# A 1-core encoder layer: four operands of the second token pair split while gate and up are computed, and other statistics at three places

## The chip, the core and the metric

The kernel runs on one core of one Trainium2 chip. The metric is the device time of one execution in microseconds (us), the median of several executions. Engines are named as in the profile: PE (TensorE), DVE (VectorE), ACT (ScalarE), POOL (GpSimd), SP (SyncE, which issues most DMAs). All arithmetic is fp32.

## What is computed

One layer of an encoder for 1088 tokens (64 of a running stream, 1024 of a new prompt), 1024 features, hidden width 2816:

```python
h = rmsnorm(x, g_mix)
z = h @ w_in                       # columns: u (512), v (512), xb (512)
ya = gelu(u) * gmlp_spatial(rmsnorm(gelu(v), g_v), w_s, b_s)
yb, new_hist = pool_mix(xb, hist, start_pos, w_pool, pool_scale)
x = x + concat(rmsnorm(ya), rmsnorm(yb)) @ w_out
h = rmsnorm(x, g_ffn)
x = x + (silu(h @ w_gate) * (h @ w_up)) @ w_down
y = rmsnorm(x, g_final)
```

`rmsnorm` divides each token by the root of its mean square over the features. The results are y, the pooling history and the normalised v of the running stream.

## The kernel before

Activations lie feature-major: 128 features on the partitions, tokens along the row. PE has no full-speed fp32 product, so every factor is split in a high part (a cast by ACT) and a low part (a subtraction by DVE), and every product is three matmuls: high x high, high x low, low x high (`passes`, L90; `products`, L659).

**Start.** L224 to L249 load x in eight feature tiles, split each, and form the sum of squares per token: ACT squares a tile (L205), POOL adds it to `sqx` (L206, `square_add`). PE computes v for six of the token tiles as x arrives, then the seventh (L249). `rstd` (L125) then sums `sqx` over the partitions with nine one-column matmuls (L128), DVE scales the sums (L130), POOL raises them to the power -1/2 (L132). Its PSUM bank is one of eight that are handed out in turn.

**Output projection.** The tokens are worked in two halves of 544 ("pairs", x = 0 and x = 1), each of two quarters of 272 (Q). After each half the second norm is made by `prep(x)` (L562), a generator whose pieces are advanced between other work: `stat` (L479: one-column matmuls L484, DVE L489, POOL power L491), `row` (L494: five transposes L497 that turn the statistic into a row along the tokens, copied out of PSUM by L498), the scaling L573, and seven operands of a Strassen-Winograd 2x2 scheme, each cast (L578) and subtracted (the helper `sub`, L471). They stand in `R0` for x = 0 and `R1` for x = 1. Order of use: B11, T1, T2, B21, T3, B22, T4; as numbers B11, T3, B21, B22 are 0 to 3, and T1, T2, T4 are 4 to 6. `R1[0..3]` are in tiles `Yh`, `Yl`.

**Gate and up.** 22 units j of 128 hidden columns (`gu_unit`). Each calls `products`, seven products of 12 matmuls per half (L678); after five of the products PSUM is read out: ACT copies (`grab`, L692), DVE adds and subtracts, ACT applies silu (L711, L716), DVE writes the result `G` (L718, L719). After every odd unit `g_operands` forms the seven operands that the down projection needs from two units and stores them in DRAM (`gd`, L731). Weights come through `load_w` (three DMAs, L613 to L615, which take three buffers "F" from `f_free`) and `steps` (DVE sums and differences of weight blocks, ACT cast L626, DVE subtraction), into pairs of buffers `w_free`; `fill` runs steps as long as a pair is free.

**Down.** The hidden pairs are summed in three groups (4, 4, 3). A group has four units q (two output tiles each); its 14 operands are fetched from `gd` (`g_load`, L819, one DMA of 544 KB each) into the low tile and split there (`g_split`, L823 by ACT and L471 by DVE). `g_next` does this for the next group, product by product, as the last unit of the group before (which is run once per half) lets each operand go. The sums are held in `accC`, `accE`, `accL`.

**End.** `finish(x)` (L914): `stat`, `row`, eight scalings L921 and eight DMAs L922.

Within each engine the order is fixed by a scheduler when the program is built; each engine runs its own instructions in that order, and SP issues its DMAs in that order too.

Of the kernel before, what the change touches and what calls it, by code (L numbers as in the profile page):

```python
# [58 lines left out]
def encoder_kernel(ctx: ExitStack, tc: tile.TileContext, xT, w_in, w_out, w_gu, w_down,  # L59
# [139 lines left out]
    def square_add(acc, x, c, first, scale=1.0):  # L199
        a, e = c  # L200
        if first:
            nc.scalar.activation(acc[:, a:e], x, AF.Square, scale=scale)
        else:
            t = tmp()
            nc.scalar.activation(t[:, 0:e - a], x, AF.Square, scale=scale)  # L205
            nc.gpsimd.tensor_tensor(out=acc[:, a:e], in0=acc[:, a:e], in1=t[:, 0:e - a], op=ALU.add)  # L206
# [21 lines left out]
    for k in range(KT):  # L228
        raw = xr[k // 4][:, k % 4]
        parts = ((0, mid), (mid, T)) if k < 2 else ((0, T),)  # L230
        if k < 2:
            nc.sync.dma_start(wr[:, k], w_in[0, 0][:, k])
        for a, e in parts:
            nc.sync.dma_start(raw[:, a:e], xT[k][:, a:e])
        if k < 2:
            split(wr, *vw[0], g_mix[:, 0:2], (k,))
        for a, e in parts:
            nc.scalar.copy(Hh[k][:, a:e], raw[:, a:e])
            nc.vector.tensor_tensor(out=Hl[k][:, a:e], in0=raw[:, a:e], in1=f(Hh[k][:, a:e]), op=ALU.subtract)
        for c in CH:  # L240
            square_add(sqacc, raw[:, c[0]:c[1]], c, k == 0)
        if k % 2 and k < 6:
            vw.append(weights(0))
        for b in first_tiles:
            passes(vps[b], tok_pairs(vw, (k,), b), k == 0, k == KT - 1)

    nc.sync.dma_start(gv_b, g_rows[0].partition_broadcast(P))
    ps = bank()
    passes(ps, tok_pairs(vw, range(KT), 7))  # L249
    vps[7] = ps  # L250
    r1 = rstd(sqacc, D, "x")
# [227 lines left out]
    def stat(sums, dim, name):  # L479

        ps = bank()
        for i, o, n in BLOCKS:
            for k, (a, at) in enumerate(sums):
                nc.tensor.matmul(ps[0:n, i:i + 1], a[:, at + o:at + o + n], ones, start=k == 0, stop=k == len(sums) - 1)  # L484
# [3 lines left out]
        for i, j, n in ((0, q - 1, P), (q - 1, q, BLOCKS[-1][2])):  # L488
            nc.vector.tensor_scalar(out=m[0:n, i:j], in0=ps[0:n, i:j], scalar1=1.0 / dim, scalar2=EPS,  # L489
# [4 lines left out]
    def row(r, out):  # L494
        R = bank2().rearrange("p a t -> p (a t)")
        for i, o, n in BLOCKS:
            nc.tensor.transpose(R[:, o:o + n], r[0:n, i:i + 1].to_broadcast([n, P]), ident[0:n, 0:n])  # L497
        nc.vector.tensor_copy(out, R[:, 0:2 * Q])  # L498

# [222 lines left out]

    def g_operands(p, xs):
# [6 lines left out]
        def store(c, v, n=2):  # L730
            nc.sync.dma_start(gd[p, c:c + n, :, a:e].rearrange("c p x t -> p c x t"), v)  # L731
# [80 lines left out]
    fill()  # L812
    make_R1()
    pieces = prep(1)


    def g_load(c, base, J, x):
        h, l = (t[:, 0:J] for t in RR[x][c])
        nc.sync.dma_start(f(l), gd[base:base + J, c, :, x].rearrange("j p t -> p j t"))  # L819
# [6 lines left out]
    def g_next(base, J, x):  # L826

        def between(c):
            g_load(c, base, J, x)
            g_split(c, J, x)  # L830
        return between

    gx = dram.tile([P, 2, Q], F32, name="gx")
    kept = []
    for i, (j, xs, how) in enumerate(units):
        if i == 3:
            for _ in pieces:
                pass
            e = big.tile([P, 2, 2, HALF], F32, tag="E", name="F")
            wx = big.tile([P, 2, 2, HALF], F32R, tag="Hl67", name="W")  # L840
            extra = [e[:, 0], e[:, 1]]
            f_free += extra
            extra_w = (wx[:, 0], wx[:, 1])
            w_free.append(extra_w)
        if i == len(units) - 5:
            retired[:] = [id(slot) for slot in extra + c_pairs]
            give(f_free, [])
# [4 lines left out]
        elif i == 2:  # L852
            gu_unit(j, xs, lambda c: next(pieces, None), kept=kept)
            nc.sync.dma_start(gx, G[1][:, :, 1])
        elif i < len(units) - 1:
            gu_unit(j, xs, lambda c: next(pieces, None), **(dict(keep=kept) if how else {}))
# [13 lines left out]
    def acc_tiles():  # L870
        c = big.tile([P, 4, T], F32, tag="C", name="accC")
        e = big.tile([P, 2, T], F32, tag="E", name="accE")
        acc[0:6] = [c[:, 0], c[:, 1], c[:, 2], c[:, 3], e[:, 0], e[:, 1]]
        for m in range(6):
            acc_load(m)

    def acc_last():
        retired[:] = [id(extra_w)]
# [35 lines left out]
    def finish(x, last):  # L914
        r = stat([(sq3, 2 * Q * x)] + [(t, 0) for t in last], D, f"o{x}")
        yield
        R = tmp2()
        row(r, R)
# [99 lines left out]
```

## Time and profile before

| | us |
|---|---|
| median of the runs shown (3) | 1036.54 |
| lowest, highest | 1034.67, 1038.34 |
| the profiled execution | 1037.52 |
| its span, first to last instruction | 1035.7 |
| PE busy | 1004.0 (97% of the span) |
| DVE, ACT, POOL busy | 649.2 (63%), 415.5 (40%), 102.8 (10%) |
| mean granted TensorE clock | 0.979 |
| bytes moved by DMA | 131.34 MB |

The page of the profile gives busy times, the span in 40 slices and the chain of work that ended last. Three other views of the same trace are used below: busy time by stage (one line for each stretch of the span), waits (which engine sat idle, until which instruction, how often, the longest), and the timeline (single instructions in order). "Busy" for PE is modelled, so that a full stretch can still run at the lower of its two clock levels, 1.2 instead of 2.4 GHz; the column PEclk, the granted clock as a share of the upper level, shows it.

### The profile page before, as it was taken

Reading aid. Unit: us, or ns where it says so; the run is one execution under the profiler, and the core shown is the slowest. Engines: PE = TensorE matmul, PEld = TensorE weight load, DVE = VectorE, ACT = ScalarE, POOL = GpSimd, SP = SyncE. Lnnn points to the kernel's source line nnn. Section 1 sums busy time; section 2 is a strip of 40 time slices with the busy share of each in tenths; the row PEclk is TensorE's granted clock in tenths of the full one; section 3 lists DMA queues with packets and bytes.
Section 4 is the critical chain, followed back from the end, with each engine's and each line's share of the span. In section 5 each row is a group of like instructions: output and inputs, shape, how many; then the busy total and the mean of one; then the engine's idle time right before and its main releaser. Section 6 shows DMA issues by size and latency. Waiting matters only on the chain.

```text
span 1035.7 us, 17622 instructions
## 1 busy us (share of the span) xinstructions
PE 1004.0 (97%) x7355; PEld 976.4 (94%) x7355; DVE 649.2 (63%) x871; ACT 415.5 (40%) x634; POOL 102.8 (10%) x117
## 2 busy tenths in 40 slices
PE   8899999999989999999999999999989998999994
PEld 7789988999989999999999999999989998999994
DVE  6658628435888455655545655455596579559855
ACT  7373435322444333333333333333473264236530
POOL 6630141112300000000000000000000000000320
PEclk9999999999989999999999999999999999999996
DMA  8211101997614231613323134153584283236104
GB/s 305 72 41 50 42 31 42 361 319 261 197 43 140 72 117 42 206 41 127 118 71 117 53 115 130 39 184 106 175 277 132 70 259 121 77 97 192 54 1 172
DMA packets 71792, 131.34 MB, mean 127 GB/s; under 512 B 7009, under 2 KB 31073, under 8 KB 71713
## 3 DMA queue, kind: packets, MB, share of 16 engines
q1 hardware_dynamic: 70560, 128.00, 37.6%
q10 hardware_dynamic: 1152, 2.23, 0.6%
q8 instruction: 57, 0.93, 0.4%
q14 instruction: 23, 0.18, 0.1%
HBM read 90.98 MB, written 39.22 MB: 126 GB/s over the span
## 4 chain that ended last, share of the span: by engine, by line
PE 87%; DVE 4%; DMA 2%; issue 1%; ACT 1%; POOL 0%; DVEq 0%; ACTq 0%
PE ps L678 63%; PE ps L95 21%; DMA R0l<-gd 1%; PE ps L484 1%; DVE Yl L471 0%; DMA R1l<-gd 0%; DVE R1l L471 0%; DVE accL L474 0%; PE ps L497 0%; PE ps L418 0%; DVE X1a L573 0%; DVE Wl L471 0%; PE ps L141 0%; ACT Yh L578 0%; ACT t L692 0%
## 5 line engine op out<-in xcount | busy, mean ns | idle before, releaser
L678 PE MATMUL ps<-R0h,Wh 128*128 128x272 f32 x624 | 182.2, 292 | 4.4 <-ACT t L692 1.8
L678 PE MATMUL ps<-R0h,Wl 128*128 128x272 f32 x624 | 180.6, 290 | 0.1
L678 PE MATMUL ps<-R0l,Wh 128*128 128x272 f32 x624 | 180.1, 289 | 0.0
L471 DVE TENSOR_TENSOR Wl<-F,Wh 128x1024 fp32r<-128x1024 f32 (+2 forms) x96 | 102.8, 1073 | 77.6 <-ACT Wh L626 77.6
L692 ACT COPY t<-ps 128x544 f32<-128x544 f32 (+1 forms) x172 | 87.7, 514 | 152.3 <-PE ps L678 149.9
L626 ACT CAST Wh<-F 128x1024 fp32r<-128x1024 f32 (+3 forms) x96 | 87.6, 912 | 148.3 <-PE ps L678 132.9
L678 PEld LDWEIGHTS ps<-R0h,Wh 128*128 128x128 f32 x624 | 118.1, 189 | 6.6 <-ACT t L692 3.8
L678 PE MATMUL ps<-R0h,W 128*128 128x272 f32 x568 | 121.2, 294 | 3.1 <-ACT t L692 3.1
L678 PEld LDWEIGHTS ps<-R0l,Wh 128*128 128x128 f32 x624 | 118.3, 190 | 0.0
L678 PEld LDWEIGHTS ps<-R0h,Wl 128*128 128x128 f32 x624 | 117.7, 189 | 0.3 <-DVE Wl L471 0.3
L545 POOL TENSOR_TENSOR sq<-sq,t 128x544 f32<-128x544 f32 x20 | 34.7, 1745 | 747.9 <-PE ps L678 670.9
L678 PE MATMUL ps<-Yh,Wh 128*128 128x272 f32 x352 | 102.6, 292 | 4.0 <-DVE G L718 2.2
L678 PE MATMUL ps<-Yh,Wl 128*128 128x272 f32 x352 | 102.2, 290 | 0.0
L678 PE MATMUL ps<-Yl,Wh 128*128 128x272 f32 x352 | 101.7, 289 | 0.0
L678 PEld LDWEIGHTS ps<-R0h,W 128*128 128x128 f32 x568 | 95.5, 193 | 3.5 <-ACT t L692 3.5
L678 PE MATMUL ps<-R1h,Wh 128*128 128x272 f32 x280 | 82.1, 293 | 1.0 <-ACT t L692 1.0
L678 PE MATMUL ps<-R0l,W 128*128 128x272 f32 x284 | 83.0, 292 | 0.0
L678 PE MATMUL ps<-R1h,Wl 128*128 128x272 f32 x280 | 81.6, 292 | 0.0
L678 PE MATMUL ps<-R1l,Wh 128*128 128x272 f32 x280 | 81.1, 290 | 0.0
L474 DVE TENSOR_TENSOR t<-ps,t 128x544 f32<-128x544 f32 (+1 forms) x50 | 32.8, 655 | 70.6 <-PE ps L678 70.6
L678 PE MATMUL ps<-Yh,W 128*128 128x272 f32 x352 | 73.6, 290 | 0.1
L471 DVE TENSOR_TENSOR F<-F 128x512 f32<-128x512 f32 (+1 forms) x105 | 71.9, 699 | 1.2
(253 smaller groups left out, 2423.4 us busy)
## 6 DMA issues: line engine op xcount, KB each, us to landing
gd<-G SPq DMA_DIRECT2D x30, 544.0 KB, 3.7
F<-in_w_gu SPq DMA_DIRECT2D x46, 256.0 KB, 2.7
F<-in_w_gu SPq DMA_DIRECT2D x23, 512.0 KB, 3.9
R0l<-gd SPq DMA_DIRECT2D x14, 544.0 KB, 5.3
raw<-in_w_in SPq DMA_DIRECT2D x11, 512.0 KB, 3.9
t<-in_xT SPq DMA_DIRECT2D x16, 272.0 KB, 4.8
Yl<-gd SPq DMA_DIRECT2D x8, 544.0 KB, 5.3
raw<-in_w_out SPq DMA_DIRECT2D x8, 512.0 KB, 5.6
```

The source lines that it names most:

```text
L95: nc.tensor.matmul(ps, a, b, start=first and i == 0, stop=last and i == n - 1)
L471: nc.vector.tensor_tensor(out=o, in0=a, in1=b, op=ALU.subtract)
L474: nc.vector.tensor_tensor(out=o, in0=a, in1=b, op=ALU.add)
L484: nc.tensor.matmul(ps[0:n, i:i + 1], a[:, at + o:at + o + n], ones, start=k == 0, stop=k == len(sums) - 1)
L545: nc.gpsimd.tensor_tensor(out=a, in0=a, in1=t, op=ALU.add)
L626: nc.scalar.copy(h, F[:, 0:k])
L678: nc.tensor.matmul(ps[:, x, 0:Q], w[:, half, k * P:(k + 1) * P], v[:, k], start=start and i == 0, stop=i == 3 * K - 1, skip_group_check=True)
L692: nc.scalar.copy(t, ps)
```

## The change

1. `square_add` works on two chunks of 544 tokens, not three of 364, 362 and 362.
2. `rstd` of x stands ahead of the seventh token tile's matmuls.
3. `stat` sums over its k sources outermost, each matmul into a column of its own; DVE then sums the columns (two TENSOR_REDUCE, L490) ahead of the scaling, which is unchanged in count. `row` is divided: `row_ps` leaves the row in PSUM, and the last `finish` reads it there, eight times, with no copy.
4. A tile `ES` takes the place of two weight buffers (`f_free` has four in place of six). From the fourth unit on, where both halves are at hand, operands 0 to 3 of half x = 1 are split by `store` as they are made (four casts, four subtractions of 272 columns for a hidden pair) and both parts are stored in a new DRAM tensor `gs`; `gd` receives their x = 0 part. At the changes of group these four are fetched already split, two DMAs of 544 KB (408 KB for the third group) in place of one DMA, one cast and one subtraction of all four (three) hidden pairs.
5. The statistic of `prep(1)` is emitted before the first unit; its seven other pieces are advanced at every second product of the first two units, not at every one. A `fill` ahead of them is gone. `accE` is allocated and loaded one unit later.

The number of matmuls of the products is unchanged.

```diff
--- before.py
+++ after.py
@@ -201,7 +201,7 @@
         if first:
             nc.scalar.activation(acc[:, a:e], x, AF.Square, scale=scale)
         else:
-            t = tmp()
+            t = tmp2()
             nc.scalar.activation(t[:, 0:e - a], x, AF.Square, scale=scale)
             nc.gpsimd.tensor_tensor(out=acc[:, a:e], in0=acc[:, a:e], in1=t[:, 0:e - a], op=ALU.add)
 
@@ -237,7 +237,7 @@
         for a, e in parts:
             nc.scalar.copy(Hh[k][:, a:e], raw[:, a:e])
             nc.vector.tensor_tensor(out=Hl[k][:, a:e], in0=raw[:, a:e], in1=f(Hh[k][:, a:e]), op=ALU.subtract)
-        for c in CH:
+        for c in ((0, 2 * Q), (2 * Q, T)):
             square_add(sqacc, raw[:, c[0]:c[1]], c, k == 0)
         if k % 2 and k < 6:
             vw.append(weights(0))
@@ -245,10 +245,10 @@
             passes(vps[b], tok_pairs(vw, (k,), b), k == 0, k == KT - 1)
 
     nc.sync.dma_start(gv_b, g_rows[0].partition_broadcast(P))
+    r1 = rstd(sqacc, D, "x")
     ps = bank()
     passes(ps, tok_pairs(vw, range(KT), 7))
     vps[7] = ps
-    r1 = rstd(sqacc, D, "x")
     prefetch(2)
 
 
@@ -479,22 +479,28 @@
     def stat(sums, dim, name):
 
         ps = bank()
-        for i, o, n in BLOCKS:
-            for k, (a, at) in enumerate(sums):
-                nc.tensor.matmul(ps[0:n, i:i + 1], a[:, at + o:at + o + n], ones, start=k == 0, stop=k == len(sums) - 1)
+        for k, (a, at) in enumerate(sums):
+            for i, o, n in BLOCKS:
+                nc.tensor.matmul(ps[0:n, 8 * k + i:8 * k + i + 1], a[:, at + o:at + o + n], ones, start=True, stop=True)
         q = len(BLOCKS)
         m = const.tile([P, q], F32, name=f"m_{name}")
         r = const.tile([P, q], F32, name=f"r_{name}")
         for i, j, n in ((0, q - 1, P), (q - 1, q, BLOCKS[-1][2])):
-            nc.vector.tensor_scalar(out=m[0:n, i:j], in0=ps[0:n, i:j], scalar1=1.0 / dim, scalar2=EPS,
+            v = ps[0:n, 0:8 * len(sums)].rearrange("p (k i) -> p i k", i=8)[:, i:j]
+            nc.vector.reduce_sum(out=m[0:n, i:j], in_=v, axis=mybir.AxisListType.X)
+            nc.vector.tensor_scalar(out=m[0:n, i:j], in0=m[0:n, i:j], scalar1=1.0 / dim, scalar2=EPS,
                                     op0=ALU.mult, op1=ALU.add)
             nc.gpsimd.tensor_tensor(out=r[0:n, i:j], in0=m[0:n, i:j], in1=mhalf[0:n, i:j], op=ALU.pow)
         return r
 
-    def row(r, out):
+    def row_ps(r):
         R = bank2().rearrange("p a t -> p (a t)")
         for i, o, n in BLOCKS:
             nc.tensor.transpose(R[:, o:o + n], r[0:n, i:i + 1].to_broadcast([n, P]), ident[0:n, 0:n])
+        return R
+
+    def row(r, out):
+        R = row_ps(r)
         nc.vector.tensor_copy(out, R[:, 0:2 * Q])
 
 
@@ -720,6 +726,11 @@
 
         products(HALF, xs, after, between, **how)
 
+
+
+    gs = dram.tile([NF // 2, 4, 2, P, Q], F32, name="gs")
+    ES = []
+
     def g_operands(p, xs):
 
         a, e = xs[0], xs[-1] + 1
@@ -728,6 +739,16 @@
         t4 = tmp2().rearrange("p (x t) -> p x t", x=2)[:, a:e]
 
         def store(c, v, n=2):
+            if ES and e == 2 and c < 4:
+                hl = ES[0][:, c // 2]
+                for i in range(n):
+                    nc.scalar.copy(hl[:, i, 0], v[:, i, 1 - a])
+                    sub(hl[:, i, 1], v[:, i, 1 - a], f(hl[:, i, 0]))
+                nc.sync.dma_start(gs[p, c:c + n].rearrange("c h p t -> p c h t"), f(hl))
+                if a:
+                    return
+                nc.sync.dma_start(gd[p, c:c + n, :, 0].rearrange("c p t -> p c t"), v[:, :, 0])
+                return
             nc.sync.dma_start(gd[p, c:c + n, :, a:e].rearrange("c p x t -> p c x t"), v)
 
         sub(G3[:, 0], G1[:, 1], G1[:, 0])
@@ -809,13 +830,17 @@
     wc = big.tile([P, 2, 2, 2, HALF], F32R, tag="C", name="W")
     c_pairs = [(wc[:, i, 0], wc[:, i, 1]) for i in range(2)]
     w_free += c_pairs
-    fill()
     make_R1()
     pieces = prep(1)
+    next(pieces)
 
 
     def g_load(c, base, J, x):
         h, l = (t[:, 0:J] for t in RR[x][c])
+        if x and c < 4:
+            for i, t in enumerate((h, l)):
+                nc.sync.dma_start(f(t), gs[base:base + J, c, i].rearrange("j p t -> p j t"))
+            return
         nc.sync.dma_start(f(l), gd[base:base + J, c, :, x].rearrange("j p t -> p j t"))
 
     def g_split(c, J, x):
@@ -827,8 +852,16 @@
 
         def between(c):
             g_load(c, base, J, x)
-            g_split(c, J, x)
+            if not x or c >= 4:
+                g_split(c, J, x)
         return between
+
+    done = [0]
+
+    def pace(c):
+        if done[0] in (0, 2, 4, 6, 8, 10, 12):
+            next(pieces, None)
+        done[0] += 1
 
     gx = dram.tile([P, 2, Q], F32, name="gx")
     kept = []
@@ -836,24 +869,22 @@
         if i == 3:
             for _ in pieces:
                 pass
-            e = big.tile([P, 2, 2, HALF], F32, tag="E", name="F")
+            ES.append(big.tile([P, 2, 2, 2, Q], F32R, tag="E", name="ES"))
             wx = big.tile([P, 2, 2, HALF], F32R, tag="Hl67", name="W")
-            extra = [e[:, 0], e[:, 1]]
-            f_free += extra
             extra_w = (wx[:, 0], wx[:, 1])
             w_free.append(extra_w)
         if i == len(units) - 5:
-            retired[:] = [id(slot) for slot in extra + c_pairs]
-            give(f_free, [])
+            retired[:] = [id(slot) for slot in c_pairs]
+            give(w_free, [])
         if i == LATER:
             gu_unit(j, xs)
             nc.sync.dma_start(G[1][:, :, 1], gx)
             g_operands(0, xs)
         elif i == 2:
-            gu_unit(j, xs, lambda c: next(pieces, None), kept=kept)
+            gu_unit(j, xs, pace, kept=kept)
             nc.sync.dma_start(gx, G[1][:, :, 1])
         elif i < len(units) - 1:
-            gu_unit(j, xs, lambda c: next(pieces, None), **(dict(keep=kept) if how else {}))
+            gu_unit(j, xs, pace, **(dict(keep=kept) if how else {}))
         else:
             kept = []
             gu_unit(j, (0,), g_next(0, GROUPS[0], 0), keep=kept)
@@ -869,12 +900,15 @@
 
     def acc_tiles():
         c = big.tile([P, 4, T], F32, tag="C", name="accC")
+        acc[0:4] = [c[:, 0], c[:, 1], c[:, 2], c[:, 3]]
+        for m in range(4):
+            acc_load(m)
+
+    def acc_last():
         e = big.tile([P, 2, T], F32, tag="E", name="accE")
-        acc[0:6] = [c[:, 0], c[:, 1], c[:, 2], c[:, 3], e[:, 0], e[:, 1]]
-        for m in range(6):
+        acc[4:6] = [e[:, 0], e[:, 1]]
+        for m in (4, 5):
             acc_load(m)
-
-    def acc_last():
         retired[:] = [id(extra_w)]
         give(w_free, [(big.tile([P, 2, HALF], F32R, tag="B3h", name="Wh"),
                        big.tile([P, 2, HALF], F32R, tag="B3l", name="Wl"))])
@@ -914,8 +948,11 @@
     def finish(x, last):
         r = stat([(sq3, 2 * Q * x)] + [(t, 0) for t in last], D, f"o{x}")
         yield
-        R = tmp2()
-        row(r, R)
+        if x:
+            R = row_ps(r)[:, 0:2 * Q]
+        else:
+            R = tmp2()
+            row(r, R)
         for m in range(KT):
             v = tokens(acc[m], x)
             nc.vector.scalar_tensor_tensor(out=v, in0=v, scalar=g_fin[:, m:m + 1], in1=R, op0=ALU.mult, op1=ALU.mult)
```

Three places of the order. The first is PE at the start, one piece of the difference between the two orders: L128 are the nine one-column matmuls of `rstd`, the L95 rows behind the first are the seventh token tile, those behind the second belong to the next stage.

```order
 L95 MATMUL ps<-wB3l,Hh_125 128x512
 L95 MATMUL ps<-wB3h,Hl_132 128x512
+L128 MATMUL ps<-ones,sqx 128x1 x9
 L95 MATMUL ps<-wB0h,Hh_118 128x512
 L95 MATMUL ps<-wB0l,Hh_118 128x512
@@ -168,5 +169,4 @@
 L95 MATMUL ps<-wB3l,Hh_125 128x512
 L95 MATMUL ps<-wB3h,Hl_132 128x512
-L128 MATMUL ps<-ones,sqx 128x1 x9
 L95 MATMUL ps<-wB0h,Hh_118 128x512
 L95 MATMUL ps<-wB0l,Hh_118 128x512
```

The nine matmuls moved ahead of the 24 of the seventh tile, so that DVE's L130 and POOL's L132 have that tile's matmuls beside them.

The second is SP's queue at the end of gate and up, as the first group's operands of x = 1 are fetched (L819 before; L844 and L842 in the change), the last hidden pair's operands are stored (L731 before; L747, L750, L752), and the weights of the second unit of the down projection are loaded (L613 to L615 before; L619 to L621). Before:

```order
L819 DMA Yl<-gd 128x4x272 x3
L819 DMA R1l_2787<-gd 128x4x272
L613 DMA F<-in_w_down 128x512
L614 DMA F<-in_w_down 128x2x512
L731 DMA gd<-G 128x2x544
L615 DMA F<-in_w_down 128x512
L731 DMA gd<-G 128x2x544
L731 DMA gd<-G_7501 128x2x544
L731 DMA gd<-t 128x544
L613 DMA F<-in_w_down 128x512
```

In the change:

```order
L842 DMA Yh<-gs 128x4x272
L842 DMA Yl<-gs 128x4x272
L844 DMA R1l_2761<-gd 128x4x272
L747 DMA gs<-ES 128x4x272
L750 DMA gd<-G 128x2x272
L747 DMA gs<-ES 128x4x272
L750 DMA gd<-G 128x2x272
L752 DMA gd<-G_7578 128x2x544
L752 DMA gd<-t 128x544
L619 DMA F<-in_w_down 128x512
L620 DMA F<-in_w_down 128x2x512
L621 DMA F<-in_w_down 128x512
```

The second unit's three weight loads stood ahead of or among the stores; they now stand behind all six, and the pair of fetches from `gs` stands there four times, once for each of the four operands, where one fetch stood.

The third is PE behind its last product. Before, the first two rows of this piece stand there four times:

```order
L484 MATMUL ps<-ones,sq_9288 128x1
L484 MATMUL ps<-ones,t 128x1 x2
L484 MATMUL ps<-ones,sq_9288 32x1
L484 MATMUL ps<-ones,t 32x1 x2
L497 MATMUL ps<-ident,r_o_10051 128x128 x4
```

and in the change:

```order
L484 MATMUL ps<-ones,sq_9367 128x1 x4
L484 MATMUL ps<-ones,sq_9367 32x1
L484 MATMUL ps<-ones,t 128x1 x4
L484 MATMUL ps<-ones,t 32x1
L484 MATMUL ps<-ones,t 128x1 x4
L484 MATMUL ps<-ones,t 32x1
L499 MATMUL ps<-ident,r_o_10132 128x128 x4
```

The rows with `t` read the squares of the last two output tiles. Only the last five of the 15 now stand behind the last of these squares; before, 13 did.

## Rows read from the trace of the kernel before

**Rows 1.** Busy time by stage: stretch, length, busy PE PEld DVE ACT POOL, granted clock, DMA share, GB/s

```profile
50.00:66.00 16.00, 15.71 (x62) 12.71 (x63) 8.41 (x14) 12.23 (x25) 6.19 (x12) 0.81 0.01 2
...
284.00:306.20 22.20, 19.09 (x143) 18.50 (x141) 17.25 (x23) 11.56 (x17) 1.90 (x2) 0.90 0.15 49
306.20:750.00 443.80, 443.79 (x3492) 443.14 (x3492) 252.48 (x339) 157.09 (x224) 0.00 (x0) 0.99 0.33 108
750.00:772.00 22.00, 17.91 (x135) 16.87 (x133) 21.10 (x25) 17.42 (x24) 0.00 (x0) 1.00 0.89 285
772.00:836.00 64.00, 64.00 (x494) 63.82 (x495) 41.95 (x61) 20.30 (x31) 0.00 (x0) 0.97 0.36 111
836.00:868.00 32.00, 28.21 (x213) 26.88 (x213) 27.23 (x35) 21.77 (x28) 0.00 (x0) 1.00 0.82 268
...
927.00:950.00 23.00, 21.42 (x166) 20.70 (x165) 19.60 (x30) 16.24 (x25) 0.00 (x0) 1.00 0.81 243
...
1015.50:1035.70 20.20, 7.15 (x42) 6.41 (x40) 10.62 (x19) 1.31 (x2) 1.52 (x2) 0.58 0.45 171
```

**Rows 2.** Waits of PE over the span: for whom, us in total, times, longest

```profile
PE ps L678 <- ACT t L692: 6.4, 6, 3.1
PE ps L678 <- DVE accL L474: 3.0, 2, 1.7
PE ps L95 <- DVE m_x L130: 2.7, 1, 2.7
PE ps L678 <- DVE G L718: 2.2, 1, 2.2
```

**Rows 3.** Timeline, PE, 40 to 52 us: start, duration, instruction, idle before it

```profile
45.53 2.06 PE L128 MATMUL ps<-ones,sqx 128*128 128x1 f32 x18
50.28 0.79 PE L95 MATMUL ps<-wB0h,Hh 128*128 128x512 f32 x1 [2.69 <-DVE m_x L130]
```

**Rows 4.** Timeline, DVE, 44 to 53 us

```profile
48.93 1.23 DVE L166 TENSOR_TENSOR raw<-raw,vec_sb 128x1024 f32<-128x1024 f32 x1 [3.52 <-DMA raw<-in_w_in]
50.07 0.16 DVE L130 TENSOR_SCALAR m_x<-ps 128x9 f32<-128x9 f32 x1
```

**Rows 5.** Instructions of L206 and L545: durations in ns min/median/max, first and last start

```profile
L206 POOL TENSOR_TENSOR sqx<-sqx,t x21: 823/1422/2022, 10.0 to 40.9; 128x362 f32<-128x362 f32 x14, 128x364 f32<-128x364 f32 x7
...
L545 POOL TENSOR_TENSOR sq<-sq,t x20: 1350/1418/6024, 195.4 to 999.3; 128x544 f32<-128x544 f32 x20
```

**Rows 6.** Timeline, POOL, 285 to 307 us

```profile
288.67 1.90 POOL L491 TENSOR_TENSOR r_f<-m_f,mhalf 128x4 f32<-128x4 f32 x2 [11.86 <-DVE m_f L489]
```

**Rows 7.** Waits of all engines, 320 to 750 us

```profile
DVE F L474 <- DMA F<-in_w_gu: 23.8, 16, 2.9
```

**Rows 8.** Timeline, DVE, SP and PE around the first change of group

```profile
765.94 1.28 DVE L471 TENSOR_TENSOR Yl<-Yl,Yh 128x1088 fp32r<-128x1088 f32 x1
...
766.61 0.46 SPq L613 DMA_DIRECT2D F<-in_w_down  x1
...
774.84 0.34 SPq L615 DMA_DIRECT2D F<-in_w_down  x1
...
777.35 0.33 SPq L731 DMA_DIRECT2D gd<-t  x1
...
790.42 0.29 PE L678 MATMUL ps<-R0h,Wh 128*128 128x272 f32 x1
```

**Rows 9.** Timeline, PE and DVE, behind the last product

```profile
1018.28 0.38 PE L484 MATMUL ps<-ones,t 128*128 128x1 f32 x2 [0.69 <-ACT t L535]
...
1022.76 0.21 DVE L489 TENSOR_SCALAR m_o<-ps 128x4 f32<-128x4 f32 x2 [3.23 <-PE ps L484]
...
1025.46 0.72 DVE L498 COPY t<-ps 128x544 f32<-128x544 f32 x1 [2.49 <-PE ps L497]
```

**Rows 10.** Groups by line and shape, 306 to 750 us: busy us, mean ns, idle before

```profile
L718 DVE TENSOR_TENSOR G<-ps,t 128x544 f32<-128x544 f32 x19 | 13.7, 720 | 0.2 <-PE ps L678 0.2
L719 DVE TENSOR_TENSOR G<-t 128x544 f32<-128x544 f32 x19 | 13.7, 719 | 0.7 <-ACT t L716 0.7
```

More of the change, by code (lines that the diff above doesn't have):

```diff
@@ L871, in acc_tiles @@
         c = big.tile([P, 4, T], F32, tag="C", name="accC")
-        e = big.tile([P, 2, T], F32, tag="E", name="accE")
-        acc[0:6] = [c[:, 0], c[:, 1], c[:, 2], c[:, 3], e[:, 0], e[:, 1]]
-        for m in range(6):
+        acc[0:4] = [c[:, 0], c[:, 1], c[:, 2], c[:, 3]]
+        for m in range(4):
             acc_load(m)
     def acc_last():
+        e = big.tile([P, 2, T], F32, tag="E", name="accE")
+        acc[4:6] = [e[:, 0], e[:, 1]]
+        for m in (4, 5):
+            acc_load(m)
         retired[:] = [id(extra_w)]
```

## The prediction

> **What bounds the kernel now.** PE does: the table gives it 1004.0 of 1035.7 us, so 31.7 us are idle. The first view to read is busy time by stage, for where they lie. Gate and up hold none: 443.79 of 443.80 us, 3492 matmuls at 0.127 us each [rows 1]. The reader is to see in the other rows that the loss sits in few places: 3.1 us around the second norm of half 1 (22.2 less 19.09), 4.1, 3.8 and 1.6 us at the three changes of operand group (at 750, 836, 927), and 13 us behind the last product [rows 1]. The second view, PE's waits, names the last releaser there: a copy by ACT (6.4 us in six waits), two adds into accL (3.0), the scaling m_x at the start (2.7), the product G (2.2) [rows 2]. The third thing is the granted clock: after an idle stretch or a run of one-column matmuls PE works on at the lower level (1.2 GHz) for a while: 0.81 over the 16 us from 50, 0.90 over the norm's 22.2, 0.97 over the 64 us behind the first change [rows 1]. That is 3.0, 2.2 and 1.9 us more which no idle time shows.
>
> The sum is made against the profiled execution, 1037.5 us, 1.0 above the median; 1.8 of it lie outside its span. Matmuls of the products stay as they are, so every gain is a gap closed.
>
> **Start (items 1, 2).** Now PE runs the nine sums (2.06 us from 45.53), then waits 2.69 us, since its next PSUM bank is the one m_x must read [rows 3]. m_x takes 0.16 us but stands on DVE behind an instruction that waited for a weight DMA until 48.93 [rows 4]. In the change 24 matmuls lie behind the sums; the 62 of the next stretch took 15.71 us at clock 0.81 [rows 1], so 24 take about 5 us at the upper level, which covers m_x. The wait goes: +2.7. What is late next is POOL's running sum: 21 adds of 1.42 us median, the last begun at 40.9 [rows 5], while PE would now ask for it at 45.5 less 5, about 40.5. Fourteen adds of 544 columns cost 1.42 each if they run as in the later stages, 2.13 if time goes by columns as at the start (1.42 x 544/363) [rows 5]: 20 to 30 us against 30 now. So PE may wait for between nothing and 1.8 us; I take 0.2, since ACT's squares (24 becoming 16) also delay POOL less. The lower clock behind the sums I leave in place: the one-column matmuls remain. **+2.5, ends 1 and 5.5** (the upper one if the clock holds as well, +3.0).
>
> The Trainium skill (GPSIMD Engine Reference, section Specifications) says that POOL shares its SBUF interface with DVE instructions that have two SBUF inputs, as the subtractions at the start do. By that rule the adds keep their price per column and the start gains 1, not 2.5, and the sum is 11.4; the trace agrees in so far as the 363-column adds there take as long as 544-column ones later (1422 and 1418 ns).
>
> **Second norm of half 1 (items 3, 5).** Now 3.1 us of idle PE end on an ACT copy [rows 2] that stands behind casts of the operands, and those behind DVE. Spread over 14 products in place of seven, they leave ACT free between; that removes the 3.1 and the low clock that follows, which I price like the one behind the 2.2 us wait at 772: 1.9. Against it: only five matmuls (0.6 us) now lie between the last sums and the transposes, and between them come DVE (two reductions and two scalings, each pair about the 0.21 of m_o [rows 9]) and POOL's 1.90 us [rows 6]. So PE waits some 2.0 to 2.2 us there. Net **+2.8, ends 0** (the operands are late all the same) **and 5.**
>
> **Gate and up (item 4).** Ten hidden pairs gain four casts and four subtractions of 272 columns; at most 0.72 us each (the 544-column form [rows 10]), 29 us for either engine, and DVE is busy 252, ACT 157 of 443.8 us [rows 1]: hidden, as long as none stands ahead of a copy that PE waits for. Two buffers fewer: a load needs three, so with six, two loads could be held, with four only one. DVE already waits 16 times for these loads, up to 2.9 us [rows 7], and PE not at all. I take **-0.3, ends -3 and 0.**
>
> **First change of group (item 4).** Lost now: 4.1 idle and 1.9 by the clock. DVE is busy 21.1 of the 22 us [rows 1]. Four subtractions of 1.28 [rows 8] go, 5.1 us, and four casts of ACT; that is more than the 2.2 us by which G comes late [rows 2]. Against it stand two things. The four operands are fetched as two DMAs each: 2.2 MB more, 7.8 us at the 285 GB/s of this stretch, where the queues are 0.89 busy [rows 1]. And the weights of the second down unit now stand on SP behind all six stores: the last store is issued at 777.35, the last weight load was at 774.84, so it comes some 3.7 us later, at 778.5; the unit begins at 790.42 [rows 8]. Of these 15.6 us, 3.7 and up to 7.8 are used up, about 3 are needed for sum, cast and subtraction: it just fits, and not if PE arrives 4 us earlier. **+1.0, ends -3 and +4.5.**
>
> **Second and third change.** At the second, 3.0 of 3.8 us wait for adds into accL [rows 2], which stand in DVE's queue among these same subtractions; 5.1 us fewer there remove them. The extra 2.2 MB take 8.3 us at 268 GB/s [rows 1], but an operand of half 1 is used 84 matmuls or 10.7 us after it is let go, and there are no stores here. **+3.0, ends 1 and 3.8.** The third loses 1.6 in all; part of it is half 0, which is untouched: **+1.0, ends 0 and 1.6.**
>
> **End (item 3).** From the last square to m_o PE needs 4.48 us for 13 of 15 sums [rows 9]. Now five stand there: 1.7, a gain of 2.8. The copy out of PSUM, 0.72 [rows 9], goes. Two reductions come in, at most 0.2 each. The eight scalings then read PSUM: a product with one PSUM operand takes 720 ns, with both in SBUF 719 [rows 10], so nothing is added. **+2.9, ends 2.2 and 3.3.** The same statistic of half 0 and of the norm before lies beside other work.
>
> The Trainium skill (VectorE: DVE Perf Modes, section Rules for kernel authors) advises to copy PSUM to SBUF first where many operations read it, since a PSUM source can cost speed. By that rule the eight readings would each be longer and the copy worth keeping: the end would gain 2.2 and the sum be 12.2. The two rows above differ by one nanosecond, so I go by them.
>
> **Sum.** 2.5 + 2.8 - 0.3 + 1.0 + 3.0 + 1.0 + 2.9 = 12.9 us: 1024.6 against the profiled execution, 1023.6 against the median. I say 1024.5.
>
> **Rivals.**
>
> A. Transfers become the bound at the changes. For it: queues 0.89 and 0.82 busy there [rows 1], 15% more bytes or more in each, the weights behind the stores. Against: the deadlines above. The first change then costs 3, the others gain nothing: 2.5 + 2.8 - 0.3 - 3 + 2.9 = 4.9, **1032.6**.
>
> B. Slower: weight loads with four buffers. If a load can start only when the unit before has used up its buffers, DVE waits for it at the head of its queue, with that unit's reading of PSUM behind it, and PE stands still once per unit. Nineteen units run with both halves [rows 10]; at 1 us each this costs 19 against 13.2 from the rest: **1043**. It decides from 13.2/19 = 0.7 us per unit. For it: DVE waits there now for up to 2.9 us [rows 7]. Against: not one of these waits reaches PE in 443.8 us [rows 1], and a unit lasts long beside a load.
>
> C. The norm of half 1 only moves its stall. The wait for POOL (2.0) is followed by the low clock (1.9) and the casts still delay one copy: the term is -2 in place of +2.8, **1029.3**. For it: five matmuls as cover. Against: ACT and DVE have twice the time for each piece.
>
> **How the numbers follow.** Forecast 0.64, C 0.14, A 0.14, B 0.08. Under about 0.3%, 3.1 us, a difference can't be told from none. The forecast, C and somewhat less than half of A are faster: 0.84. The rest of A and a mild B are the same: 0.10. B is slower: 0.06. The terms' ends taken as independent (about 6 us either way, the first change and the norm the widest) give 1018.5 to 1031; taken on to most of A, 1018.5 to 1032.5. That leaves out B and the tails, under 0.2.
>
> **What the profile would show.** Right: no wait of PE for m_x, and m_x before the seventh tile ends; a wait of about 2 us for r_f near 288 and none near 303; no wait for accL at the second change; m_o 2.5 us closer to the last square, and no copy behind the last transposes. Wrong: PE below 443 of 443.8 us busy in gate and up with DVE's F as releaser (B); a PE wait at the second down unit for its weights (A); the granted clock under 0.9 after the norm (C).

## The result and the profile after

The change takes 1025.2 us, median of four runs (1023.07 to 1026.13), against 1036.24 (1034.67 to 1038.34): 0.9889 of before, 95% interval 0.9865 to 0.9913, 11.0 us less. A second set of six runs gave 1026.7 and 0.9913 (0.9895 to 0.9931). The profiled execution of the change took 1026.13 us, with a span of 1024.4. The forecast was 1024.5 in 1018.5 to 1032.5. One run of those told of below counts as slow, 1955.7 us of no_presplit, and is left out of every figure.

Busy time by stage of the change, same stretches and columns as [rows 1]; as work is done up to 11 us earlier, the late stretches hold later work than the same ones of before:

```profile
50.00:66.00 16.00, 16.00 (x84) 13.94 (x83) 9.97 (x14) 13.11 (x28) 6.80 (x14) 1.00 0.01 3
...
284.00:306.20 22.20, 21.69 (x139) 21.04 (x139) 15.93 (x24) 10.42 (x16) 1.90 (x2) 0.77 0.14 37
306.20:750.00 443.80, 442.06 (x3496) 440.78 (x3495) 267.13 (x382) 173.41 (x267) 0.00 (x0) 1.00 0.37 120
750.00:772.00 22.00, 20.93 (x161) 20.08 (x160) 20.04 (x28) 14.53 (x25) 0.00 (x0) 1.00 1.09 368
772.00:836.00 64.00, 62.28 (x479) 61.75 (x478) 37.43 (x53) 19.57 (x29) 0.00 (x0) 0.97 0.45 145
836.00:868.00 32.00, 31.54 (x244) 30.65 (x243) 26.47 (x39) 18.32 (x27) 0.00 (x0) 1.00 0.95 323
...
927.00:950.00 23.00, 22.72 (x179) 22.28 (x178) 18.95 (x34) 12.90 (x23) 0.00 (x0) 1.00 0.79 260
```

And PE's waits, as in [rows 2]:

```profile
PE ps L95 <- DVE Hl L239: 2.0, 2, 1.7
PE ps L684 <- ACT Wh L632: 1.7, 2, 1.5
PE ps L684 <- DVE t L474: 1.6, 2, 1.3
PE ps L499 <- POOL r_o L493: 1.6, 1, 1.6
...
PE ps L684 <- ACT t L698: 1.3, 3, 0.9
```

All the waits of [rows 2] are gone or short: none for m_x, none for accL, none for G. New are chiefly one for a weight cast (1.5 us, at 784.65) and two for t (1.6 us, at 313 and 316). In 50 to 66 us PE ran 84 matmuls in place of 62, at clock 1.00. But in 284 to 306 the clock is 0.77 where it was 0.90. In the stretch behind that it is the other way round, before:

```profile
306.20:320.00 13.80, 13.79 (x86) 13.60 (x87) 13.32 (x20) 5.36 (x9) 0.00 (x0) 0.78 0.26 77
```

and in the change:

```profile
306.20:320.00 13.80, 12.20 (x93) 11.56 (x92) 13.80 (x21) 5.46 (x9) 0.00 (x0) 1.00 0.10 31
```

To see where the 11.3 us of span went, both traces are cut at the same instructions: the end of the output projection's last matmul; the start of the fourth and the 23rd product G that DVE reads from PSUM; of the 9th, 25th, 45th and last addition from PSUM into acc; the end. "Again" is the second profile of the change.

| stretch | before | change | again | forecast gain | gain |
|---|---|---|---|---|---|
| start to output projection | 283.9 | 281.4 | 281.2 | 2.5 | 2.5, 2.7 |
| norm of half 1, first units | 65.4 | 65.1 | 65.1 | 2.8 | 0.3, 0.3 |
| gate and up | 392.5 | 392.5 | 392.6 | -0.3 | 0.0, -0.1 |
| first change of group | 70.0 | 69.3 | 69.1 | 1.0 | 0.7, 0.9 |
| second | 81.1 | 77.2 | 77.2 | 3.0 | 3.9, 3.9 |
| third | 85.9 | 84.7 | 86.2 | 1.0 | 1.2, -0.3 |
| last unit with finish(0) | 38.2 | 39.6 | 38.7 | 0 | -1.4, -0.5 |
| end | 18.7 | 14.7 | 15.0 | 2.9 | 4.0, 3.7 |

The sum came out near the forecast partly because errors cancel: the norm gave 2.5 too little, finish(0) lost up to 1.4 that was not priced, the second change and the end gave 0.9 and 1.1 too much. Part of it is also the clock, which differs between traces of one order of instructions. The experiments ask why.

### The profile page after: what moved, and what is told of

Same layout as the page of the kernel before. It is cut to its first block, busy times and chain, and to the rows that moved or that the text cites. A ratio compares the mean times of both kernels' runs of the same rounds, so it can differ in the third digit from the quotient of the medians.

```text
span 1024.4 us, 17705 instructions
## 1 busy us (share of the span) xinstructions
PE 1003.2 (98%) x7355; PEld 974.9 (95%) x7355; DVE 655.9 (64%) x910; ACT 419.0 (41%) x658; POOL 100.6 (10%) x110
## 2 busy tenths in 40 slices
DMA packets 88688, 143.60 MB, mean 140 GB/s; under 512 B 7520, under 2 KB 53088, under 8 KB 88608
## 4 chain that ended last, share of the span: by engine, by line
PE 85%; DVE 7%; DMA 3%; ACT 2%; issue 2%; POOL 1%; SPq 0%; DVEq 0%; ACTq 0%; POOLq 0%
PE ps L684 63%; PE ps L95 19%; DMA R0l<-gd 1%; PE ps L484 1%; DVE Hl L239 1%; DMA R1l<-gd 1%; DVE R1l L471 1%; DMA xrC<-in_xT 1%; ACT ps L262 1%; DVE X1a L471 0%; POOL r_v L149 0%; DVE t L265 0%; PE ps L499 0%; ACT Wh L632 0%; PE ps L418 0%
## 5 line engine op out<-in xcount | busy, mean ns | idle before, releaser
L632 ACT CAST Wh<-F 128x1024 fp32r<-128x1024 f32 (+2 forms) x96 | 87.1, 912 | 129.0 <-PE ps L684 115.7
L684 PE MATMUL ps<-R0h,W 128*128 128x272 f32 x568 | 118.7, 290 | 0.0
L684 PEld LDWEIGHTS ps<-R0h,W 128*128 128x128 f32 x568 | 93.3, 188 | 0.2 <-ACT t L698 0.2
L684 PEld LDWEIGHTS ps<-Yh,Wh 128*128 128x128 f32 x352 | 66.8, 190 | 0.5 <-ACT t L698 0.5
```

What stands on the lines that cost most here:

```text
L632: nc.scalar.copy(h, F[:, 0:k])
L684: nc.tensor.matmul(ps[:, x, 0:Q], w[:, half, k * P:(k + 1) * P], v[:, k], start=start and i == 0, stop=i == 3 * K - 1, skip_group_check=True)
```

## The experiments

All edits are to the changed kernel. Stretches are those of the table.

**no_presplit.** The split at the store is undone: `ES` stays empty, the two weight buffers come back, and the tests on it become

```diff
-        if x and c < 4:
+        if ES and x and c < 4:
...
-            if not x or c >= 4:
+            if not (ES and x and c < 4):
```

> The change without its item 4: no split at the store, no gs, two more weight buffers as before; items 1, 2, 3, 5 stay. Theory (the split at the store earns what the changes of group gained: 0.8 + 3.9 + 1.2 = 5.9 us in the trace): total 1031 (1029.5 to 1032.5), PE waits for accL and G at 768 and near 860 come back, gate and up unchanged within 0.5. Rival 1 (the changes of group gain by something else, such as the later accE load or the four weight buffers): total stays within 1024 to 1027. Rival 2 (the split costs gate and up something that the trace hides): gate and up become shorter by 1 or more, total 1029 or less.

1030.2 us (ratio 0.9951, 0.9934 to 0.9969). The three changes took 69.7, 81.0 and 86.4 us, in sum 5.9 more than in the first trace of the change; gate and up 391.8, that is 0.7 less. PE's waits of that kernel from 740 to 960 us:

```profile
PE ps L684 <- DVE accL L474: 3.0, 2, 1.6
PE ps L684 <- ACT t L698: 2.6, 7, 0.6
PE ps L684 <- DVE G L724: 2.2, 1, 2.2
```

The totals for accL and G are those of [rows 2], to the tenth. The theory holds: the four operands that arrive split take their subtractions out of DVE's queue, and the additions into accL, and G, are no longer late. The second change shows it best (81.1 before, 81.0 here, 77.2 in the change); the third differs here by little more than between two traces of the change. The 0.7 us in gate and up is near the 1 us of rival 2, but the kernel before, which has no such split either, took 392.5 there.

**late_store.** The last hidden pair's operands are formed and stored behind the first run of the first down unit:

```diff
-        if j % 2 and how < 2:
+        if j % 2 and how < 2 and i < len(units) - 1:
             g_operands(j // 2, xs)
...
                     down_unit(q, J, (x,), nxt, **how)
+                    if gi == 0 and q == 0 and x == 0:
+                        g_operands(NF // 2 - 1, (0, 1))
```

> The change with the last hidden pair's operands formed and stored after the first run (half 0) of the first down unit, so that SP issues the second unit's three weight loads ahead of the six stores. Theory (the 1.5 us wait of PE at 784.6 for a weight cast and the 2 us of lower clock behind it come from the loads standing behind the stores): the wait goes, the first change gains 3 to 4 us more, total 1021 to 1022.5. Rival (the weights are late by the transfers, 2.2 MB more at full queues, wherever the loads stand): the wait stays at 1 us or more, total 1024 to 1025.5.

1019.9 us (0.9853, 0.9823 to 0.9883). The first change took 64.6 us, not 69.3. SP, DVE and PE of the change's first profile, timeline:

```profile
771.93 0.84 SPq L752 DMA_DIRECT2D gd<-t  x1
772.81 1.18 SPq L619 DMA_DIRECT2D F<-in_w_down  x1
...
782.48 0.69 DVE L474 TENSOR_TENSOR F<-F 128x512 f32<-128x512 f32 x1
...
784.65 0.39 PE L684 MATMUL ps<-R0h,Wh 128*128 128x272 f32 x1 [1.53 <-ACT Wh L632]
```

The same rows of late_store, where PE has no such wait:

```profile
762.23 2.40 SPq L619 DMA_DIRECT2D F<-in_w_down  x1
...
774.04 0.69 DVE L474 TENSOR_TENSOR F<-F 128x512 f32<-128x512 f32 x1
```

The loads leave 10 us sooner, the sum of the weights on DVE comes 8 us sooner (1.9 of each were won ahead of this stage), and PE reaches the second unit without a stop; the bytes are the same, so it was the place in the queue and in DVE's order (the edit moves the stores and the forming of their operands together, and does not tell the two apart). In the change the load was even in time: its row at 782.48 shows no wait for a DMA, but it stands behind additions that wait for PE. What is late is its place in DVE's order, which is fixed when the program is built.

Not all of the 4.7 us is that place. The 1.53 us wait for the cast stands in ten traces. In six of them the granted clock over this stretch is 0.975, and it took 68.8 to 69.8 us; in the four others (sums_old_mid, three_chunks, copy_back, end_old_sums) it is 1.00 and the stretch took 67.4 to 67.9. So some 3 us are the place of the loads, and the rest is a lower clock that does not always follow the wait. Of the total, some 2 us more lie at the norm (63.0 in place of 65.1), which this edit does not touch.

**pace_each.** `pace` advances a piece at every one of the first seven products, as before.

> The change with the seven pieces of the second norm of half 1 advanced at every product, as before, the statistic still ahead of the units. Theory A (the clock after the sums decides): the 3 us idle stretch near 303 comes back, the norm stretch is longer by 2 to 4, total 1027 to 1029; the pacing is worth that, and it is the sums that take it away. Theory B (the pacing only moves the stall): total within 1024 to 1026, an idle stretch near 303 in place of the waits at 313 to 317.

1025.3 us (0.9907, 0.9874 to 0.9941): the same as the change. The idle time near 303 is back, 2.5 us for an ACT copy at 304.73, and the two waits for t are gone; the stretch took 65.3. By the total this is theory B: the pacing moves the stall, at the same price. But the two traces differ in their clock, behind the sums as well as behind the copy. late_store, which is paced as the change is, has the clock of pace_each behind the sums:

```profile
284.00:306.20 22.20, 21.08 (x156) 20.53 (x155) 17.82 (x28) 12.22 (x18) 1.90 (x2) 0.92 0.13 37
306.20:320.00 13.80, 12.18 (x93) 11.55 (x92) 13.80 (x20) 4.92 (x8) 0.00 (x0) 1.00 0.20 66
```

pace_each:

```profile
284.00:306.20 22.20, 18.57 (x133) 17.90 (x133) 18.52 (x26) 11.59 (x16) 1.89 (x2) 0.92 0.12 37
306.20:320.00 13.80, 13.80 (x97) 13.54 (x96) 13.65 (x23) 5.52 (x10) 0.00 (x0) 0.88 0.25 82
```

late_store took 63.0 us there. With the clock behind the sums alike, the wider pacing is worth 2.3 us: 0.9 of idle time (2.5 against 1.6) and the lower clock behind the copy.

**no_sums.** The norm of half 1 takes the statistic of half 0:

```diff
+    kept_r = []
...
-        r = stat(sums[x], D, f"f{x}")
+        if x == 0:
+            kept_r.append(stat(sums[x], D, "f0"))
+        r = kept_r[0]
```

> The change without the statistic of the norm of half 1: it takes over the one of half 0 (30 one-column matmuls, two reductions, two scalings and the two powers are left out; the transposes stay). Theory (the one-column sums are what lowers the clock there): the granted clock stays above 0.95 from 280 to 300 us, the stretch from the end of the output projection to the fourth G falls from 63 to 66 us to 56 to 59. Rival (the clock falls by what DVE and ACT delay, or by chance): it falls all the same, and the stretch is 60 to 62, that is 3.5 for the sums and 0.5 to 1 for the wait for POOL.

1019.2 us (0.9845, 0.9814 to 0.9876); the stretch took 58.0 us. Busy time in stretches of 4 us, columns as in [rows 1]. The change:

```profile
284.00:288.00 4.00, 4.00 (x22) 3.97 (x22) 0.68 (x4) 0.39 (x1) 0.22 (x1) 0.55 0.01 4
288.00:292.00 4.00, 3.49 (x15) 2.87 (x14) 2.06 (x5) 1.04 (x1) 1.67 (x2) 0.50 0.46 117
292.00:296.00 4.00, 4.00 (x25) 4.00 (x24) 3.62 (x5) 1.12 (x3) 0.00 (x0) 0.67 0.27 79
```

late_store, which has the same order on PE here:

```profile
284.00:288.00 4.00, 3.12 (x26) 2.87 (x25) 1.62 (x6) 0.40 (x2) 1.21 (x1) 1.00 0.02 4
288.00:292.00 4.00, 3.76 (x17) 3.46 (x18) 2.44 (x3) 1.03 (x1) 0.68 (x2) 0.58 0.49 131
292.00:296.00 4.00, 4.00 (x34) 4.00 (x33) 3.56 (x7) 2.42 (x4) 0.00 (x0) 1.00 0.21 68
```

no_sums:

```profile
284.00:288.00 4.00, 4.00 (x34) 4.00 (x33) 4.00 (x6) 1.72 (x3) 0.00 (x0) 1.00 0.43 131
288.00:292.00 4.00, 4.00 (x34) 4.00 (x33) 3.81 (x6) 3.37 (x5) 0.00 (x0) 1.00 0.22 68
```

Without the 30 one-column matmuls the clock stays at 1.00 and 7.1 us go, as the theory had it. That the sums lower the clock is not shown by this, for three later traces have the sums, in the same order on PE, and keep the clock. three_chunks, copy_back and end_old_sums:

```profile
284.00:306.20 22.20, 21.08 (x164) 20.45 (x164) 20.54 (x30) 12.23 (x18) 1.90 (x2) 1.00 0.17 48
284.00:306.20 22.20, 21.09 (x167) 20.66 (x166) 18.96 (x29) 12.23 (x18) 1.90 (x2) 1.00 0.17 48
284.00:306.20 22.20, 21.09 (x168) 20.60 (x168) 18.14 (x28) 12.24 (x19) 1.89 (x2) 1.00 0.17 50
```

Their stretch took 62.1 us each. So of the 7.1 us 4.1 are the sums and the wait for POOL behind them (62.1 less 58.0), and 3.0 are the lower clock (65.1 less 62.1). In the change it comes while PE is full (4.00 of 4.00 us in the first row), behind the first 20 sums (281.20 to 283.44) and around the last ten (285.39 to 287.29), so an idle PE is not what brings it on there; the sums are the likely cause, but they do not bring it on each time. How long it stays low differs too: in the change the sums begin at 281.20, and PE runs 22, 15 and 25 matmuls in these stretches; in late_store they begin at 281.42 in the same order, and it runs 26, 17 and 34. What decides between these traces stays open.

**sums_old_mid, twice, after_again and both.** The sums as before (source innermost, no reductions) everywhere but in the last finish; the change again as a control; both edits, sums_old_mid and late_store, together.

> The change with the sums as before (source innermost, no reductions) everywhere but in the last finish. Theory A (the sums with the source outermost, run in two bunches with products between, put PE on the lower clock earlier and longer: 0.77 after against 0.90 in 284 to 306 us, 0.71 against 0.90 in 999 to 1015.5): the norm of half 1 gains 1.5 to 3, the stretch of finish(0) 1.4, total 1021 to 1022.5. Theory B (the loss at the norm is PE's two waits for t at 313 to 317, 1.6 us, from where the pieces stand): these waits stay, the norm stretch is as in the change within 0.5, total 1024 to 1025.5.

> The kernel with the old sums everywhere but at the end, again, beside the control on one chip. Theory A (the new sums cost clock in the middle): 2.5 to 4 us below the control. Theory C (the 3.7 us of the first time were the clock's spread): within 1.5 us of the control.

> The changed kernel itself, once more, as the control for the next two: 1024 to 1026.5 if the first four runs were typical. In the runs so far the same order of instructions took 63.0 to 66.1 us around the norm of half 1 and 38.1 to 40.2 us around finish(0), so these two stretches of this trace should again differ from the first one's 65.1 and 39.6 by up to 2 us each (theory C: where the clock falls is not set by the order alone). Rival: they repeat within 0.3.

> Old sums in the middle and the last pair's stores behind the weight loads. If A and the theory on the stores hold: 1016 to 1018. If only the stores matter: 1019 to 1021.

1021.5 (0.9867, 0.9832 to 0.9902) the first time; 1023.5 (0.9887, 0.9860 to 0.9914) the second, beside 1026.7 of the control; both together 1020.3 (0.9854, 0.9831 to 0.9876), no better than late_store alone. The norm took 64.6, 63.7 and 63.7 us with the old sums, and finish(0) 38.2, 38.2 and 39.9. With the new sums in this same order the norm took 65.1, 65.1, 66.1, 63.0, 65.1, 62.1, 62.1 and 62.1 us (change, control, no_presplit, late_store, rstd_behind, three_chunks, copy_back, end_old_sums), and finish(0) 38.1 to 40.2. Each follows the granted clock of its stretch. The norm: 62.1 us at 1.00, 63.0 at 0.97, 65.1 and 66.1 at 0.92, and with the old sums 63.7 and 64.6 at 0.95. finish(0): 38.1 to 38.7 at 0.955, 39.6 to 40.2 at 0.91. Theory A predicted a fixed price and is not shown; theory C fits these spreads, though the same kernel repeated its norm stretch exactly (65.1 twice, with sums from 281.20 and 281.02), against C's expectation; finish(0) differed by 0.9. The totals, 3 to 4 us below the change twice but no gain in "both", go with the clock as well: 0.982 to 0.987 in the ten runs of the change, 0.982 to 0.992 in the ten with the old sums. Whether the old sums hold the clock up, or it fell less often by chance, is open.

**three_chunks and rstd_behind.** The start's two parts, each undone alone: the squares in three chunks again (`CH`, `tmp`), or `rstd` behind the seventh tile again.

> The change with the squares of x added in three chunks as before; the sums still ahead of the seventh tile. In the change the 14 adds took 2.08 us each at the median, as long per column as the 21 before. Theory (the chunks are worth nothing, the place of the sums all): the second statistic's matmuls (those on Y) begin at 144 to 145 us as in the change (144.4; 147.2 before). Rival (POOL is late without the wider chunks): PE waits 1 us or more ahead of the first one-column matmul, the second statistic begins at 145.5 or later.

> The change with the sums of x behind the seventh tile as before; two wide chunks stay. Theory: PE's wait of 2.7 us for m_x and the low clock from 50 to 56 come back, the second statistic begins near 147. Rival: with fewer adds DVE and POOL are earlier, the wait is under 1 us, and the second statistic begins at 145.5 or earlier.

Instructions of L128, L206 and L239 (DVE's subtraction that splits x): duration in ns min/median/max, first and last start. The change:

```profile
L128 PE MATMUL ps<-ones,Y x18: 164/250/250, 144.4 to 146.2; 128*128 128x1 f32 x18
...
L206 POOL TENSOR_TENSOR sqx<-sqx,t x14: 1362/2084/2424, 10.4 to 36.5; 128x544 f32<-128x544 f32 x14
...
L239 DVE TENSOR_TENSOR Hl<-xrAl,Hh x4: 2444/2450/2457, 22.3 to 35.3; 128x1088 fp32r<-128x1088 f32 x4
```

three_chunks:

```profile
L128 PE MATMUL ps<-ones,Y x18: 164/250/250, 142.5 to 144.3; 128*128 128x1 f32 x18
...
L206 POOL TENSOR_TENSOR sqx<-sqx,t x21: 821/1423/2025, 10.3 to 41.3; 128x362 f32<-128x362 f32 x14, 128x364 f32<-128x364 f32 x7
...
L239 DVE TENSOR_TENSOR Hl<-xrAl,Hh x4: 1909/2057/2061, 20.8 to 32.9; 128x1088 fp32r<-128x1088 f32 x4
```

rstd_behind: 147.9 for the first of these matmuls; PE waits 3.07 us for m_x, and the granted clock from 50 to 66 is 0.81 again. It is 1.00 there in the twelve traces without that wait, though the nine sums stand in all of them: here the lower clock comes with the wait. The place of the sums is worth 3.5 us there (147.9 less 144.4) and earns the whole gain; the wide chunks cost 1.9 (144.4 less 142.5). POOL's adds take nearly as long per column as before (3.8 ns against 3.9 at the median; 28.3 us in all against 31.8 in three_chunks), and DVE's splits beside them 2.45 us, not 2.06. The Trainium skill (GPSIMD Engine Reference, section Specifications) says that POOL's SBUF interfaces are shared with VectorE, in contention with DVE instructions that have two SBUF inputs. These rows agree, and show the price on both sides: a DVE subtraction of 1088 columns took 1.28 us at the first change of group [rows 8], and a POOL add 2.6 ns per column later [rows 5]. In all, three_chunks took 1020.9 us in two runs (0.9837, 0.9797 to 0.9877); 3.0 of its gain over the change lie at the norm and 1.9 at the first change, which the edit does not touch and where the clock is 1.00 in its trace. rstd_behind took 1030.7 (0.9925, 0.9896 to 0.9954).

**copy_back and end_old_sums.** At the end: the row copied out of PSUM again, or the old sums in the last finish alone.

> The change with the row copied out of PSUM in the last finish too. Theory (PSUM as an operand costs the scalings nothing): the eight scalings take as long as in the change (5.6 us from the first to the last start plus 0.7), the copy adds 0.7, so from the last add into accL to the end 15.0 to 15.8 us instead of 14.0 to 15.3. Rival: the scalings from SBUF are shorter by 0.05 us or more each and the copy pays, under 14.7.

> The change with the old sums in the last finish alone (source innermost, no reductions). Theory: 13 of 15 sums stand behind the last square again; from that last add to m_o 5.3 to 5.8 us instead of 3.0, the end longer by 2.4 to 2.8. Rival (the reductions eat the gain): the end longer by less than 1.5.

The change, timeline of DVE:

```profile
1012.69 0.23 DVE L490 TENSOR_REDUCE m_o<-ps 128x4 f32<-128x12 f32 x2 [0.51 <-PE ps L484]
...
1015.61 2.86 DVE L958 SCALAR_TENSOR_TENSOR accC<-accC,vec_sb,ps 128x544 f32<-128x544 f32 x4 [2.50 <-PE ps L499]
```

copy_back:

```profile
1011.15 0.73 DVE L504 COPY t<-ps 128x544 f32<-128x544 f32 x1 [2.50 <-PE ps L499]
1011.91 2.87 DVE L955 SCALAR_TENSOR_TENSOR accC<-accC,vec_sb,t 128x544 f32<-128x544 f32 x4
```

Four scalings take 2.86 us from PSUM and 2.87 from SBUF; the copy is 0.76 for nothing, and the end took 15.9. The Trainium skill (VectorE: DVE Perf Modes, section Rules for kernel authors) advises to copy PSUM to SBUF first where many operations follow. For these eight it costs. With the old sums the last add into acc and m_o lie 4.7 us apart (1008.78 to 1013.48), against 3.0 in the change (1009.66 to 1012.69): worth 1.7, less than forecast, the end 16.1. The whole runs took 1024.3 (0.9870, 0.9821 to 0.9919) and 1027.1 us (0.9896, 0.9868 to 0.9925).

## Why the prediction was right, point by point

The total is right partly by luck: the second change and the end held by their mechanism, the start by other terms than forecast, and what was too much there made good most of the misses at the norm and at finish(0).

- **Start, 2.5 forecast, 2.5 measured, by other terms.** The wait for m_x went (2.7), and with it the lower clock: 1.00 from 50 to 66, which I had left in place because the one-column matmuls remain. Against that the wide chunks cost 1.9, where I had them help a little: the lower end of the term, POOL by the column, was nearly right, and DVE's side of it was missing. Of the 1.9, 0.75 us are waits near 73, for the splits of v, that three_chunks does not have. That it is 2.5 to the tenth is luck: with this start the output projection ended at 279.5 to 283.4 in eleven traces; the first of the matmuls on Y is steadier, 144.0 to 144.8, against 147.2 before.
- **Norm of half 1, 2.8 forecast, 0.3 measured: the step that failed.** The 3.1 us idle went, as said, and the wait for POOL was even smaller (0.5, not 2). Two new waits for t, 1.6 us, are operands made during later products, much as rival C had it. What failed is the term for the lower clock. It put the clock's loss behind the idle time, and that part went: 0.78 to 1.00 over 306.20 to 320, 3.0 us. The part behind the sums it left out: 2.2 us before (0.90 over 284 to 306.20), 5.1 in the change (0.77). The loss is thus the same 5 us in both traces, and C's sign, the clock under 0.9 after the norm, came true. But the change does not fix this part. In three traces of the same order it is nothing and the stretch took 62.1, a gain of 3.3; over the eight traces the gain is -0.7 to 3.3. The forecast of 2.8 lies within that, and the 0.3 of the first trace and of the control is their clock.
- **Gate and up, -0.3 forecast, 0 measured.** The mechanism of rival B is there and reaches no one: DVE's waits for the loads rose from 23.8 us [rows 7] to 43.7 (18 waits, the longest 3.7; 24.2 in no_presplit), and the stretch is the same 392.5 us.
- **First change, 1.0 forecast, 0.7 and 0.9 measured.** As worked out: G is no longer late (the first addition into accC starts at 769.21, not 777.23: 8.0 us sooner, 2.9 of them won earlier), and what was gained is lost again where the weights come too late, 1.5 us of idle time and the lower clock behind it. PE reached the second unit 5.8 us sooner (784.65, not 790.42), more than the 4 us up to which I had it just fit; the wait is rival A's sign, but by the order in two queues and not by the transfers. Putting it right gave 4.7, some 3 of it by the order alone.
- **Second and third change, 3.0 and 1.0 forecast, 3.9 and between -0.3 and 1.2 measured.** At the second the mechanism was right; PE's waits of the change come to 0.4 us from 835 to 960, so the 0.7 us for a copy in half 0's run, which I had left standing, went too. The third is within what its stretch varies between kernels (84.7 to 86.4, 85.9 before): its gain is not shown.
- **End, 2.9 forecast, 3.7 to 4.0 measured.** 2.7 come ahead of m_o, 0.5 from there to the first scaling; a further 0.7 lies behind the first scaling (9.5 us to the end before, 8.8 after), though the scalings are as long as they were: the last stores landed sooner, which I can't trace to the change. Of the 2.7, the order of the sums alone is 1.7 (end_old_sums); the rest goes with the clock at which they ran (from the last add to m_o the new sums took 2.6 us at 1.00 and 3.7 at 0.61). The term's own parts add up to 3.1 (2.8 and 0.7, less 0.4), not 2.9.
- **finish(0), priced at nothing,** lost 1.4 and 0.5 us; over all traces it took 38.1 to 40.2, under the same order of instructions in most. In seven, the one before among them, the clock of the stretch is 0.955 and it took 38.1 to 38.7; in the seven others it is 0.91, and 39.6 to 40.2. That is the clock's spread and not a cost that I can pin to the edit.

## What to carry to other kernels

Where DVE's queue is full, move the splitting of an operand to a stage in which DVE idles, even at the price of more bytes (143.60 MB moved, 131.34 before); then look which load stands behind the new stores, since a queue's order can be worth as much as the work that was moved (4.7 us here, some 3 with the clock alike). A gap that is closed takes the lower clock behind it along (0.81 to 1.00 at the start, 0.78 to 1.00 at the norm), but not the one that comes with a run of one-column matmuls, and that one differs from trace to trace: compare traces with the same clock in the stretch, or several of each kernel, before a difference of 3 us there is put down to an edit. Widening work on POOL shortens it little when it pays nearly by the column, and it slows DVE beside it.

## What the runs showed of the hardware

One and the same order on PE around a statistic took 62.1 to 66.1 us in eight traces of seven kernels, with the granted clock between 284 and 296 us at 0.55, 0.50, 0.67 in one, at 1.00, 0.58, 1.00 in another whose sums began 0.2 us later, and at 1.00 throughout in three. The shortest version run is late_store, 1019.9 us (0.9823 to 0.9883 of before, 0.9865 to 0.9913 for the change); "both" (1020.3) and three_chunks (1020.9) can't be told from it. late_store and three_chunks touch different stages and were not run together.
